# A layer kernel on one Trainium2 core: in fifteen of its seven-product pairs one matmul is made in two of fewer columns, or the third product comes second

## The chip, the cores and the metric

The kernel runs on one core of one Trainium2 chip. The metric is device time in microseconds (us). The kernel before was run three times without a profile: 875.72, 879.99 and 881.25 us, median 879.99. One more execution was profiled; the rows shown here are from that one.

A core has five engines that run side by side and wait for each other by semaphores: TensorE (PE in the profile) multiplies, VectorE (DVE) and ScalarE (ACT) work element by element, GpSimd (POOL) does small things and issues some DMAs, SyncE (SP) issues most DMAs. TensorE's work has two kinds of instruction: a weight load (PEld) puts a 128x128 block into the array, and the matmul behind it streams its columns through that block. A load runs beside the matmul before it.

## The reference, cut to what matters

A decoder layer on 512 tokens, 1024 wide: a feed-forward half step, a token mixer, a second feed-forward half step, a final norm.

```
x = x + 0.5 * swiglu_ffn(rmsnorm(x, ffn1_norm), w_gate1, w_up1, w_down1)
x = x + hybrid_mixer(rmsnorm(x, mix_norm), ...)
x = x + 0.5 * swiglu_ffn(rmsnorm(x, ffn2_norm), w_gate2, w_up2, w_down2)
y = rmsnorm(x, final_norm)

def swiglu_ffn(x, w_gate, w_up, w_down):      # w_gate, w_up: 1024 x 2816
    return (jax.nn.silu(x @ w_gate) * (x @ w_up)) @ w_down
```

Only `x @ w_gate` and `x @ w_up` are touched by the change.

## The kernel before

Every float32 operand of a product is split in a high and a low part, and a product is made as high*high + high*low + low*high. All matmuls have a 128x128 stationary block and 256 or 512 moving columns.

The 2816 features of a feed-forward step are 22 columns of 128, j = 0 to 21. Columns 0 and 1 (and 2 in the first step) are made plainly. For each later j the gate block and the up block together are a *pair*, and `seven_units` (line 452) makes the pair's four quarter results (two results, two halves of 256 tokens) in 7 half-size products instead of 8, by Strassen's scheme: sums of weight blocks (`block_hi`) by sums of token blocks (`sums`). Each product is one call of `mm_block` (line 310), 3 x 4 = 12 matmuls of 256 columns, so a pair has 84. The products go into three PSUM banks, in this order (B.., T. are weights, A.., S. token blocks):

```
("x","B11","A11"), ("z","T1","S1"), ("x","T2","S2"), ("w","B21","A12"),
("z","B22","S4"), ("x","T3","S3"), ("x","T4","A22")
```

Bank x is written by B11, and ScalarE then copies it out (`m1`, line 473) before T2 may add to it. In the same way ScalarE copies bank z (`m5`, line 477) between T1 and B22, and bank x again (`u2`, line 480) between T2 and T3. `c11`, `c12`, `c22`, `c21` add the pieces and apply silu (line 497 is `c21`'s).

`ffn` (line 940) strings the pairs together in three groups of 8, 8 and 6 columns. Each group ends with its down projection (`down_a_units`, banks pd, 512-column matmuls; the last group's is `down_b_units` or `final`). The pairs with 7 products are j = 3 to 21 in the first step and j = 2 to 21 in the second: 39 in all. `put(m[:6], 2)` lists a pair's first two products, then the last product (T4) of the pair before, then the other four. The last T4 of a group comes behind the first piece of the down projection.

The order of the instructions on each engine is a scheduler's: it takes units in the order of `run` and may move ready ones ahead of one that it believes will wait. ScalarE does, besides the copies, the casts of the weights to their high part (`slab_hi`, `block_hi`, lines 203 and 238), 1.05 us each for a whole block. VectorE makes the low parts (line 212) and the weight sums (lines 226 to 230).

Of the kernel before, what the change touches and what calls it, by code (L numbers as in the profile page):

```python
# [8 lines left out]
F32 = mybir.dt.float32  # L9
# [4 lines left out]
P = 128  # L14
# [4 lines left out]
T = 512  # L19
# [3 lines left out]
HT = 256  # L23
# [4 lines left out]
PLAIN = (3, 2)  # L28
BESIDE = (5, 9, 11, 13, 15, 18, 20)
ASIDE = 16  # L30
TAPS = 31
PR_NORM = 800
PR_CONV = -50
# [39 lines left out]
def layer_kernel(ctx: ExitStack, tc, x, gains, w_g1, w_u1, w_d1a, w_d1b, w_in,  # L73
                 chan, w_a, w_x, w_out, w_g2, w_u2, w_d2a, w_d2b, out):
    nc = tc.nc
    V, S, G, PE = nc.vector, nc.scalar, nc.gpsimd, nc.tensor
# [3 lines left out]
    sp = ctx.enter_context(tc.tile_pool(name="sp", bufs=2))  # L80
# [5 lines left out]
    def nm(s):  # L86
        uid[0] += 1
        return f"{s}_{uid[0]}"
# [4 lines left out]
    def bank(name):  # L93
        return pb.tile([P, T], F32, name=nm(name), tag="pb")
# [42 lines left out]
    def dve(us):  # L137
        clock["dve"] = max(clock["dve"], clock["pe"] - 3.0) + us
# [41 lines left out]
    def hl_tile(off):  # L180
        hl = wp.tile([P, 2 * D + 64], F32R, name=nm("hl"), tag="hl", bufs=HL_BUFS)
        return hl[:, off:off + 2 * D]
# [34 lines left out]
    def block_hi(s):  # L217
# [17 lines left out]
        n = HALF if s.kind == "b22" else D  # L235
        hl = hl_tile(ASIDE)
        s.hi, s.lo = hl[:, 0:n], hl[:, D:D + n]
# [69 lines left out]

    def mm_block(ps, b, a, first):  # L310
        (whi, wlo), (hhi, hlo) = b, a
        for i, (w, h) in enumerate(((whi, hhi), (whi, hlo), (wlo, hhi))):
            for k in range(4):
                PE.matmul(ps[:, 0:HT], w[:, k * P:(k + 1) * P], h[:, k, :],  # L314
                          start=(first and i == 0 and k == 0), stop=(i == 2 and k == 3),
                          skip_group_check=not first)

    pinned = [False]

# [100 lines left out]
    def ffn_units(acts, j, g, u_, parts):  # L420
        off = ASIDE if len(parts) == 2 else 0
        sg_, su_ = Slab(g, off=off), Slab(u_, off=off)
        box = {}

        def product(key, s, t0, n):
            box[key] = bank("p" + key)
            mm_feat(box[key][:, :n], s, t0, n)

        def gate_out(t0, n):
            box["s"] = sp.tile([P, T], F32, name=nm("sg"), tag="sg", bufs=2)  # L430
            S.activation(box["s"][:, :n], box["gate"][:, :n], AF.Silu)

        def up_out(t0, n):
            s, a = box["s"], acts[j]
            V.tensor_mul(s[:, :n], box["up"][:, :n], s[:, :n])
            S.copy(a[:, 0, t0:t0 + n], s[:, :n])
            V.tensor_sub(a[:, 1, t0:t0 + n], s[:, :n], a[:, 0, t0:t0 + n].bitcast(F32))
            dve(0.8 if n == 256 else 1.3)

        out_ = []  # L440
        for t0, n in parts:
            us = 5.44 * n / 512
            out_.append(Unit([sg_], us, lambda t0=t0, n=n: product("gate", sg_, t0, n),
                             lambda t0=t0, n=n: gate_out(t0, n), n == T))
            out_.append(Unit([su_], us, lambda t0=t0, n=n: product("up", su_, t0, n),
                             lambda t0=t0, n=n: up_out(t0, n), n == T))
        return out_
# [1 line left out]

    def seven_units(acts, j, g, u_, q):
        pair = {"gate": g, "up": u_}
        bg, bt, b2, bt2 = (Block(pair, k) for k in ("g", "t12", "b22", "t34"))
        right = {"B11": (bg, 0), "B21": (bg, 1), "T1": (bt, 0), "T2": (bt, 1), "B22": (b2, 0),
                 "T3": (bt2, 0), "T4": (bt2, 1)}
        box = {}
        h0, h1 = slice(0, HT), slice(HT, T)

        def product(to, b, a, first):  # L460
            if first:
                box[to] = bank("p" + to)
            blk, i = right[b]
            sl = slice(i * HALF, (i + 1) * HALF)
            mm_block(box[to], (blk.hi[:, sl], blk.lo[:, sl]), q[a], first)

        def evac(to, fn):
            with tc.high_priority(offset=PR_OUT):
                fn(box[to][:, 0:HT])

        def m1(ps):
            box["s"] = sp.tile([P, T], F32, name=nm("sg"), tag="sg", bufs=2)
            S.copy(box["s"][:, h0], ps)  # L473

        def m5(ps):
            box["m"] = sp.tile([P, T], F32, name=nm("um"), tag="um", bufs=2)
            S.copy(box["m"][:, h1], ps)

        def u2(ps):
            S.copy(box["m"][:, h0], ps)  # L480

        def c11(ps):
            V.tensor_add(box["s"][:, h0], ps, box["s"][:, h0])
            S.activation(box["s"][:, h0], box["s"][:, h0], AF.Silu)
            dve(0.42)

        def c12(ps):
            V.tensor_add(box["m"][:, h0], ps, box["m"][:, h0])
            dve(0.42)

        def c22(ps):
            V.tensor_add(box["m"][:, h1], ps, box["m"][:, h1])  # L492
            dve(0.42)

        def c21(ps):
            s, a = box["s"], acts[j]
            S.activation(s[:, h1], ps, AF.Silu)
            V.tensor_mul(s, s, box["m"])
            S.copy(a[:, 0, :], s)
            V.tensor_sub(a[:, 1, :], s, a[:, 0, :].bitcast(F32))  # L500
            dve(1.4)

        units = []
        for to, b, a, first, fn in (("x", "B11", "A11", True, m1), ("z", "T1", "S1", True, m5),
                                    ("x", "T2", "S2", False, u2), ("w", "B21", "A12", True, c11),
                                    ("z", "B22", "S4", False, c12), ("x", "T3", "S3", False, c22),
                                    ("x", "T4", "A22", False, c21)):
            units.append(Unit([right[b][0]], 1.41,
                              lambda to=to, b=b, a=a, first=first: product(to, b, a, first),
                              lambda to=to, fn=fn: evac(to, fn)))  # L510
        return units
# [86 lines left out]
    def zc_units(c, parts):  # L598
        off = ASIDE if len(parts) == 2 else 0
        sgt, sv = Slab(split=ws_in[4 + c], off=off), Slab(split=ws_in[c], off=off)  # L600
# [30 lines left out]
    def conv_out(c):  # L631
        return cv.setdefault(c // 2, slot([P, 2, T], "cv"))[:, c % 2, :]
# [15 lines left out]
    def conv_dve(c):  # L648
        acc, o = [bank("pc"), bank("pc")], conv_out(c)
        for j in range(TAPS):  # L650
            src, to = mx["ub"][:, c, j:j + T], acc[j % 2]
# [6 lines left out]
            else:  # L658
                V.scalar_tensor_tensor(out=o if j == TAPS - 2 else to, in0=src,  # L659
                                       scalar=par(c, P_DW + j), in1=to,  # L660
# [7 lines left out]
    def conv_pool(c):  # L668
        acc, o = slot([P, 2, T], "ca"), conv_out(c)
        for j in range(0, TAPS, 2):  # L670
            n = min(2, TAPS - j)
            to = acc if j == 0 else slot([P, 2, T], "cm")
# [248 lines left out]
    def do(fn):  # L921
        return [Unit([], 0.0, fn)]
# [13 lines left out]
    q1, q2 = {"name": "q1"}, {"name": "q2"}  # L936

    def ffn(a0, wg, wu, wd, q, plain, between=()):  # L940
        us, late, acts = [], [], [a0] + [Acts() for _ in GROUPS[1:]]
        js = iter(range(FT))

        def put(more, n):
            us.extend(more[:n] + late + more[n:])
            late.clear()

        ready = False
        for gi, n in enumerate(GROUPS):
            for i in range(n):  # L950
                j = next(js)
                if j < 2:
                    continue
                if j < plain:
                    put(ffn_units(acts[gi], i, wg[j], wu[j], [ALL]), 1)
                    continue
                if not ready:
                    us.extend(wait(q["name"]))
                    ready = True
                m = seven_units(acts[gi], i, wg[j], wu[j], q)  # L960
                m[4].aside = j in BESIDE
                if j == FT - 1:
                    put([m[k] for k in (0, 1, 2, 3, 5, 4, 6)], 1)
                else:
                    put(m[:6], 2)
                    late.append(m[6])
            if gi < 2:
                put(down_a_units(wd[gi], acts[gi], n), 1)
            if gi == 0:
                us.extend(between)  # L970
        assert not late
        return us, acts[2]

    for_later = [w_in[i] for i in range(16)] + [w_out[i] for i in range(8)]
    a1, a2 = Acts(), Acts()
    e = early_units(a1, w_g1, w_u1, wait("h11"))
    u = e[:1] + do(rest_of_x) + e[1:]
    u += do(lambda: sides.append(split_ahead(for_later, ws_in + ws_out)))
    f1, b1 = ffn(a1, w_g1, w_u1, w_d1a, q1, PLAIN[0], do(mixer_params))
    u += f1  # L980
    u += down_b_units(w_d1b, b1, then(2))
    u += do(mixer_inputs)
# [5 lines left out]
        (PR_NORM, norm_chain((t,), gains_of[3], f"h3{t // 2}" if t % 2 else None, q2))))  # L988
    u += wait("h30")
    u += early_units(a2, w_g2, w_u2, wait("h31"))  # L990
    f2, b2 = ffn(a2, w_g2, w_u2, w_d2a, q2, PLAIN[1])
    u += f2


# [105 lines left out]
```

## Time and profile before

| | us |
|---|---|
| three runs, median (lowest to highest) | 879.99 (875.72 to 881.25) |
| the profiled execution, its own time | 878.23 |
| its span, first to last instruction | 876.4 |
| PE busy in the span | 845.7 (96%) |
| DVE busy | 637.0 (73%) |
| ACT busy | 425.2 (49%) |

The rest of the time beside the span is 1.8 us. PE's busy time is that of matmul records that overlap each other (a 256-column matmul has a record of 0.28 us, and the next one starts 0.11 to 0.12 us after it). So the pace, start to start, is read from the starts of groups of matmuls in the timeline or from their count in a stretch, not from the busy share.

The program in the profile's time: first step 14 to 348 us, mixer 348 to 518, second step 518 to 836, end. The pairs with 7 products stand at 51 to 99, 144 to 221 and 266 to 328 us (first step) and at 551 to 609, 654 to 732 and 777 to 835 us (second step); between them are the down projections.

### The profile page before, as it was taken

The numbers are of one execution on the slowest core, as the hardware profiler recorded it, in microseconds if no ns is written. First come the engines' busy times: TensorE is split into PE (matmuls) and PEld (weight loads), VectorE is DVE, ScalarE is ACT, GpSimd is POOL, SyncE is SP. The second block draws the span as 40 slices with busy tenths as digits, with TensorE's granted clock in tenths as the row PEclk, the third lists the DMA queues.
The fourth block names the chain that finished last, engine by engine and source line by source line (L and its number), as shares of the span: only waits on it lengthen the run. The fifth ranks groups of instructions, "written<-read, shape, count | busy, mean of one in ns | idle before, by whom it ended". The sixth has DMA issues, their size and how long they took to land.

```text
span 876.4 us, 13745 instructions
## 1 busy us (share of the span) xinstructions
PE 845.7 (96%) x5568; PEld 768.7 (88%) x5568; DVE 637.0 (73%) x899; ACT 425.2 (49%) x677; POOL 89.7 (10%) x112
## 2 busy tenths in 40 slices
PE   7999999999998999999995999999999999999996
PEld 5999987999887998898783789999889999899985
DVE  5989655998666992659988569797547995558844
ACT  7656533656433661436652535555215654135633
POOL 2000011000111000209830010000000000000001
PEclk9999999999999999999998999999999999999998
DMA  7544689555898467555442021234312335223212
GB/s 273 162 134 170 220 309 334 193 193 170 304 325 306 145 230 275 207 202 191 145 156 84 4 93 49 95 104 134 127 49 96 101 117 164 77 73 97 102 44 96
DMA packets 36721, 139.12 MB, mean 159 GB/s; under 512 B 5041, under 2 KB 5169, under 8 KB 33970
## 3 DMA queue, kind: packets, MB, share of 16 engines
q1 hardware_dynamic: 29170, 112.04, 37.8%
q0 software_dynamic: 6912, 25.17, 7.5%
q10 hardware_dynamic: 576, 1.05, 0.3%
q8 instruction: 43, 0.70, 0.3%
q14 instruction: 20, 0.16, 0.1%
HBM read 110.98 MB, written 27.26 MB: 158 GB/s over the span
## 4 chain that ended last, share of the span: by engine, by line
PE 70%; issue 15%; DVE 5%; DMA 4%; ACT 3%; POOL 2%; SPq 0%; POOLq 0%; ACTq 0%; DVEq 0%
PE px L314 19%; PE pz L314 10%; PE pz L305 7%; PE pw L314 5%; PE pd L521 5%; PE pd L520 5%; PE pd L522 5%; PE pgate L305 3%; PE pup L305 3%; DVE pc L659 2%; DMA sraw<-in_w_out 2%; PE po L520 1%; PE po L521 1%; PE po L522 1%; PE pdl L521 1%
## 5 line engine op out<-in xcount | busy, mean ns | idle before, releaser
L212 DVE TENSOR_TENSOR hl<-raw,hl 128x1024 fp32r<-128x1024 f32 (+1 forms) x132 | 139.7, 1062 | 45.4 <-ACT hl L203 33.3
L314 PE MATMUL px<-sx,hl 128*128 128x256 f32 x936 | 122.7, 281 | 6.4 <-ACT sg L473 6.4
L314 PE MATMUL pz<-sx,hl 128*128 128x256 f32 x936 | 121.6, 280 | 0.0
L314 PEld LDWEIGHTS px<-sx,hl 128*128 128x128 f32 x936 | 115.3, 190 | 6.9 <-ACT sg L473 6.9
L520 PE MATMUL pd<-hl,act 128*128 128x512 f32 x304 | 118.7, 390 | 0.0
L521 PE MATMUL pd<-hl,act 128*128 128x512 f32 x304 | 118.4, 390 | 0.0
L522 PE MATMUL pd<-hl,act 128*128 128x512 f32 x304 | 118.4, 389 | 0.0
L212 DVE TENSOR_TENSOR hl<-tt,hl 128x1024 fp32r<-128x1024 f32 x78 | 94.9, 1217 | 30.3 <-ACT hl L238 30.3
L314 PEld LDWEIGHTS pz<-sx,hl 128*128 128x128 f32 x936 | 114.4, 189 | 0.0
L314 PE MATMUL px<-h_hi,hl 128*128 128x256 f32 x624 | 98.0, 280 | 0.0
L238 ACT CAST hl<-tt 128x1024 fp32r<-128x1024 f32 x78 | 81.8, 1052 | 27.8 <-PE pd L522 18.4
L314 PEld LDWEIGHTS px<-h_hi,hl 128*128 128x128 f32 x624 | 84.3, 189 | 1.2 <-DVE um L492 0.6
L203 ACT CAST hl<-raw 128x1024 fp32r<-128x1024 f32 x54 | 56.1, 1052 | 53.0 <-PE pd L522 42.3
L238 ACT CAST hl<-raw 128x1024 fp32r<-128x1024 f32 x78 | 65.1, 835 | 31.8 <-PE pd L522 26.3
L522 PEld LDWEIGHTS pd<-hl,act 128*128 128x128 f32 x304 | 57.1, 188 | 11.8
L520 PEld LDWEIGHTS pd<-hl,act 128*128 128x128 f32 x304 | 57.1, 188 | 11.5
L521 PEld LDWEIGHTS pd<-hl,act 128*128 128x128 f32 x304 | 57.1, 188 | 11.4
L305 PE MATMUL pz<-h_hi,hl 128*128 128x512 f32 (+1 forms) x320 | 64.9, 352 | 0.0
L305 PEld LDWEIGHTS pz<-h_hi,hl 128*128 128x128 f32 x320 | 51.8, 188 | 9.2 <-issue 1.9
L659 DVE SCALAR_TENSOR_TENSOR pc<-sx,ch,pc 128x512 f32<-128x512 f32 x84 | 56.9, 748 | 0.0
L291 DVE TENSOR_TENSOR slo<-sraw,shi 128x1024 fp32r<-128x1024 f32 x24 | 29.3, 1220 | 33.9 <-ACT shi L290 33.9
L290 ACT CAST shi<-sraw 128x1024 fp32r<-128x1024 f32 x24 | 25.2, 1051 | 52.7 <-DMA sraw<-in_w_in 30.3
(181 smaller groups left out, 1346.5 us busy)
## 6 DMA issues: line engine op xcount, KB each, us to landing
raw<-in_w_g SPq DMA_DIRECT2D x44, 512.0 KB, 3.6
raw<-in_w_u SPq DMA_DIRECT2D x44, 512.0 KB, 3.6
hl<-wsi SPq DMA_DIRECT2D x16, 1024.0 KB, 4.8
sraw<-in_w_in SPq DMA_DIRECT2D x16, 512.0 KB, 6.2
wsi<-shi POOLq DMA_DIRECT2D x16, 512.0 KB, 4.7
wsi<-slo POOLq DMA_DIRECT2D x16, 512.0 KB, 5.1
raw<-in_w_d1a SPq DMA_DIRECT2D x16, 512.0 KB, 4.3
raw<-in_w_d2a SPq DMA_DIRECT2D x16, 512.0 KB, 3.5
```

What stands on the lines that cost most here:

```text
L203: S.copy(s.hi, s.raw)
L212: V.tensor_sub(s.lo, s.raw, s.hi.bitcast(F32))
L238: S.copy(s.hi, s.raw)
L290: S.copy(hi, raws[-1])
L291: V.tensor_sub(lo, raws[-1], hi.bitcast(F32))
L305: PE.matmul(ps, w[:, k, :], h[:, k, t0:t0 + n], start=(i == 0 and k == 0), stop=(i == 2 and k == KT - 1))
L314: PE.matmul(ps[:, 0:HT], w[:, k * P:(k + 1) * P], h[:, k, :], start=(first and i == 0 and k == 0), stop=(i == 2 and k == 3), skip_group_ch ...
L520: PE.matmul(ps, ahi, whi, start=first, stop=False)
L521: PE.matmul(ps, ahi, wlo, start=False, stop=False)
L522: PE.matmul(ps, alo, whi, start=False, stop=last)
L659: V.scalar_tensor_tensor(out=o if j == TAPS - 2 else to, in0=src, scalar=par(c, P_DW + j), in1=to, op0=ALU.mult, op1=ALU.add)
```

## The change

`ffn` gets a table that names, by j, what is done in that pair. A number from 32 to 192 is a *cut*: in the pair's first product (B11) the second matmul (k = 1 of the first four) is made in two, the first with that many columns, the second with the rest of the 256; each has its own weight load of the same block. A 0 is a *swap*: the third product of the list, T2, is listed second, ahead of T1. There are 3 cuts and 1 swap in the first step, 8 cuts and 3 swaps in the second. The function `um` only lets whichever of `m5` and `u2` comes first make their tile.

```diff
+CUTS = ({3: 128, 4: 64, 5: 0, 6: 192},
+        {2: 0, 3: 192, 4: 128, 5: 64, 8: 64, 10: 32, 11: 0, 13: 128, 16: 128, 18: 0, 19: 64})
...
-    def mm_block(ps, b, a, first):
+    def mm_block(ps, b, a, first, cut=None):
         (whi, wlo), (hhi, hlo) = b, a
         for i, (w, h) in enumerate(((whi, hhi), (whi, hlo), (wlo, hhi))):
             for k in range(4):
-                PE.matmul(ps[:, 0:HT], w[:, k * P:(k + 1) * P], h[:, k, :],
-                          start=(first and i == 0 and k == 0), stop=(i == 2 and k == 3),
-                          skip_group_check=not first)
+                edges = [0, cut, HT] if cut and i == 0 and k == 1 else [0, HT]
+                for c0, c1 in zip(edges, edges[1:]):
+                    PE.matmul(ps[:, c0:c1], w[:, k * P:(k + 1) * P], h[:, k, c0:c1],
+                              start=(first and i == 0 and k == 0), stop=(i == 2 and k == 3),
+                              skip_group_check=not first)
...
-            mm_block(box[to], (blk.hi[:, sl], blk.lo[:, sl]), q[a], first)
+            mm_block(box[to], (blk.hi[:, sl], blk.lo[:, sl]), q[a], first,
+                     cut if b == "B11" else None)
...
+        def um():
+            if "m" not in box:
+                box["m"] = sp.tile([P, T], F32, name=nm("um"), tag="um", bufs=2)
+            return box["m"]
+
         def m5(ps):
-            box["m"] = sp.tile([P, T], F32, name=nm("um"), tag="um", bufs=2)
-            S.copy(box["m"][:, h1], ps)
+            S.copy(um()[:, h1], ps)
...
-                m = seven_units(acts[gi], i, wg[j], wu[j], q)
+                cut = cuts.get(j)
+                m = seven_units(acts[gi], i, wg[j], wu[j], q, cut)
                 m[4].aside = j in BESIDE
+                if cut == 0:
+                    m[1], m[2] = m[2], m[1]
```

A cut on TensorE, first step, pair 3 (the first row is the last matmuls of the plain column 2; px_73 is bank x, h_hi and h_lo the token block A11). Before:

```order
L305 MATMUL pup_66_546<-h_hi_76,hl_48_400 128x512 x8
L314 MATMUL px_73_588<-h_hi_76,hl_50_433 128x256 x4
L314 MATMUL px_73_588<-h_lo_77,hl_50_433 128x256 x4
L314 MATMUL px_73_588<-h_hi_76,hl_50_433 128x256 x4
L314 MATMUL pz_76_606<-sx0_52_461,hl_56_472 128x256 x12
```

and changed:

```order
L309 MATMUL pup_66_546<-h_hi_76,hl_48_400 128x512 x8
L320 MATMUL px_73_588<-h_hi_76,hl_50_433 128x256
L320 MATMUL px_73_588<-h_hi_76,hl_50_433 128x128 x2
L320 MATMUL px_73_588<-h_hi_76,hl_50_433 128x256 x2
L320 MATMUL px_73_588<-h_lo_77,hl_50_433 128x256 x4
L320 MATMUL px_73_588<-h_hi_76,hl_50_433 128x256 x4
L320 MATMUL pz_76_607<-sx0_52_461,hl_56_472 128x256 x12
```

One matmul of 256 columns became two of 128; nothing else moved here.

The swap on TensorE, first step, pair 5 (px_99 is its bank x, pz_102 or pz_105 its bank z; px_85 is bank x of pair 4, whose last product T4 is the rows from h_hi and h_lo into px_85; sx0 is S1, sx1 is S2). Before:

```order
L314 MATMUL px_99_815<-h_hi_76,hl_91_741 128x256 x4
L314 MATMUL px_99_815<-h_lo_77,hl_91_741 128x256 x4
L314 MATMUL px_99_815<-h_hi_76,hl_91_741 128x256 x4
L314 MATMUL pz_102_832<-sx0_52_461,hl_93_760 128x256 x12
L314 MATMUL px_85_692<-h_hi_76,hl_83_673 128x256 x4
L314 MATMUL px_85_692<-h_lo_77,hl_83_673 128x256 x4
L314 MATMUL px_85_692<-h_hi_76,hl_83_673 128x256 x4
L314 MATMUL px_99_815<-sx1_53_464,hl_93_760 128x256 x12
```

and changed:

```order
L320 MATMUL px_99_817<-h_hi_76,hl_91_743 128x256 x4
L320 MATMUL px_99_817<-h_lo_77,hl_91_743 128x256 x4
L320 MATMUL px_99_817<-h_hi_76,hl_91_743 128x256 x4
L320 MATMUL pz_105_868<-sx0_52_461,hl_93_762 128x256
L320 MATMUL px_85_693<-h_hi_76,hl_83_674 128x256 x3
L320 MATMUL px_99_817<-sx1_53_464,hl_93_762 128x256 x12
L320 MATMUL px_85_693<-h_hi_76,hl_83_674 128x256
L320 MATMUL px_85_693<-h_lo_77,hl_83_674 128x256 x4
L320 MATMUL px_85_693<-h_hi_76,hl_83_674 128x256 x4
L320 MATMUL pz_105_868<-sx0_52_461,hl_93_762 128x256 x11
```

Before, 24 matmuls stood between the end of B11 and T2, which needs ScalarE's copy of B11's result; now 4 do (one of T1, three of T4). The other swaps look the same, but for the second step's first pair, where there is no T4 yet and the four are of T1.

ScalarE at the same pair (sg_100<-px_99 is `m1`, um<-px_99 is `u2`, um<-pz is `m5`, the ACTIVATE is silu of pair 4's T4). Before:

```order
L473 COPY sg_100_828<-px_99_815 128x256
L477 COPY um_103_845<-pz_102_832 128x256
L497 ACTIVATE sg_86_705<-px_85_692 128x256
L238 CAST hl_105_864<-raw_84_689 128x1024
L499 CAST act_104_859<-sg_86_705 128x512
L480 COPY um_103_845<-px_99_815 128x256
```

and changed:

```order
L480 COPY sg_100_830<-px_99_817 128x256
L491 COPY um_102_846<-px_99_817 128x256
L508 ACTIVATE sg_86_707<-px_85_693 128x256
L242 CAST hl_104_865<-raw_84_690 128x1024
L510 CAST act_103_860<-sg_86_707 128x512
L488 COPY um_102_846<-pz_105_868 128x256
```

The copies of bank x and of bank z changed places around the silu and the two casts. VectorE, GpSimd and SyncE have the same instructions in the same order; TensorE has 11 matmuls and 11 loads more.

## Rows read from the trace of the kernel before

**Rows 1.** The page: span, busy time by engine, PE and its clock in 40 slices.

```profile
span 876.4 us, 13745 instructions
PE 845.7 (96%) x5568; PEld 768.7 (88%) x5568; DVE 637.0 (73%) x899; ACT 425.2 (49%) x677; POOL 89.7 (10%) x112
...
PE   7999999999998999999995999999999999999996
...
PEclk9999999999999999999998999999999999999998
```

**Rows 2.** Windows over the seven-product stretches (first column, us); columns in the first row.

```profile
core 0: us, PE busy (x) PEld busy (x) DVE busy (x) ACT busy (x) POOL busy (x), PEclk, DMA share, GB/s
51.20:98.80 47.60, 47.60 (x406) 47.60 (x405) 40.55 (x73) 30.76 (x51) 1.06 (x2) 1.00 0.40 132
150.20:220.00 69.80, 69.80 (x618) 69.80 (x618) 66.30 (x98) 44.62 (x76) 3.19 (x6) 1.00 0.56 193
278.40:317.60 39.20, 39.20 (x348) 39.20 (x347) 36.51 (x55) 24.45 (x42) 1.06 (x2) 1.00 0.45 152
551.60:608.00 56.40, 56.40 (x481) 56.40 (x481) 45.79 (x68) 33.17 (x58) 0.00 (x0) 1.00 0.30 95
654.60:732.00 77.40, 77.40 (x660) 77.40 (x659) 63.73 (x94) 45.68 (x78) 0.00 (x0) 1.00 0.32 102
777.40:832.00 54.60, 54.60 (x466) 54.60 (x465) 43.83 (x64) 31.38 (x55) 0.00 (x0) 1.00 0.29 98
```

**Rows 3.** Timeline of PE, 144 to 152.5 us: start, us, engine, line, tile, count, [idle before].

```profile
144.00 0.39 PE L522 MATMUL pd<-hl,act 128*128 128x512 f32 x1
144.22 0.64 PE L314 MATMUL px<-h_hi,hl 128*128 128x256 f32 x4
...
145.63 1.58 PE L314 MATMUL pz<-sx,hl 128*128 128x256 f32 x12
149.33 1.65 PE L314 MATMUL px<-sx,hl 128*128 128x256 f32 x12 [2.12 <-ACT sg L473]
150.82 0.62 PE L314 MATMUL pw<-h_hi,hl 128*128 128x256 f32 x4
...
152.18 0.50 PE L314 MATMUL pz<-sx,hl 128*128 128x256 f32 x3
```

**Rows 4.** Timeline of PE, 328 to 331 us.

```profile
328.89 0.40 PE L521 MATMUL pd<-hl,act 128*128 128x512 f32 x1
329.21 0.74 PE L314 MATMUL px<-h_hi,hl 128*128 128x256 f32 x4
329.79 0.62 PE L314 MATMUL px<-h_lo,hl 128*128 128x256 f32 x4
...
330.70 0.40 PE L522 MATMUL pd<-hl,act 128*128 128x512 f32 x1
330.93 0.40 PE L520 MATMUL pd<-hl,act 128*128 128x512 f32 x1
```

**Rows 5.** Chain that ended last: start, us, engine, bank, line, matmuls in the piece.

```profile
21.74 2.72 PE pgate L305 x24
25.33 2.83 PE pup L305 x24
```

**Rows 6.** Timeline of PE's weight loads, 24 to 25.4 us (128-column transposes, then 256-column matmuls).

```profile
24.20 0.89 PEld L348 LDWEIGHTS ptr<-ident,xn 128*128 128x128 f32 x8
25.06 0.42 PEld L305 LDWEIGHTS pup<-h_hi,hl 128*128 128x128 f32 x3
```

**Rows 7.** Timeline of all engines, 683.5 to 692.5 us (second step, pair 11).

```profile
683.68 0.64 PE L314 MATMUL px<-h_hi,hl 128*128 128x256 f32 x4
...
684.15 1.58 PE L314 MATMUL pz<-sx,hl 128*128 128x256 f32 x12
...
684.40 0.37 ACT L473 COPY sg<-px 128x256 f32<-128x256 f32 x1 [1.83 <-PE px L314]
...
686.50 0.64 PE L314 MATMUL px<-h_hi,hl 128*128 128x256 f32 x4
686.97 1.58 PE L314 MATMUL px<-sx,hl 128*128 128x256 f32 x12
687.17 0.38 ACT L497 ACTIVATE sg<-px 128x256 f32<-128x256 f32 x1 [1.04 <-PE px L314]
687.45 1.04 ACT L238 CAST hl<-raw 128x1024 fp32r<-128x1024 f32 x1
...
688.91 0.38 ACT L480 COPY um<-px 128x256 f32<-128x256 f32 x1
```

**Rows 8.** Timeline of ACT, 148 to 150 us: the copy that the matmul at 149.33 waits for.

```profile
148.92 0.36 ACT L473 COPY sg<-px 128x256 f32<-128x256 f32 x1
```

More of the change, by code (lines that the diff above doesn't have):

```diff
@@ L447, in ffn_units, with seven_units @@
         return out_
-    def seven_units(acts, j, g, u_, q):
+    def seven_units(acts, j, g, u_, q, cut=None):
         pair = {"gate": g, "up": u_}
@@ L473, in m1 @@
             S.copy(box["s"][:, h0], ps)
+        def um():
+            if "m" not in box:
+                box["m"] = sp.tile([P, T], F32, name=nm("um"), tag="um", bufs=2)
+            return box["m"]
         def m5(ps):
-            box["m"] = sp.tile([P, T], F32, name=nm("um"), tag="um", bufs=2)
-            S.copy(box["m"][:, h1], ps)
+            S.copy(um()[:, h1], ps)
         def u2(ps):
-            S.copy(box["m"][:, h0], ps)
+            S.copy(um()[:, h0], ps)
         def c11(ps):
@@ L936, in layer_kernel, with ffn @@
     q1, q2 = {"name": "q1"}, {"name": "q2"}
-    def ffn(a0, wg, wu, wd, q, plain, between=()):
+    def ffn(a0, wg, wu, wd, q, plain, cuts, between=()):
         us, late, acts = [], [], [a0] + [Acts() for _ in GROUPS[1:]]
@@ L978, in layer_kernel @@
     u += do(lambda: sides.append(split_ahead(for_later, ws_in + ws_out)))
-    f1, b1 = ffn(a1, w_g1, w_u1, w_d1a, q1, PLAIN[0], do(mixer_params))
+    f1, b1 = ffn(a1, w_g1, w_u1, w_d1a, q1, PLAIN[0], CUTS[0], do(mixer_params))
     u += f1
@@ L990, in layer_kernel @@
     u += early_units(a2, w_g2, w_u2, wait("h31"))
-    f2, b2 = ffn(a2, w_g2, w_u2, w_d2a, q2, PLAIN[1])
+    f2, b2 = ffn(a2, w_g2, w_u2, w_d2a, q2, PLAIN[1], CUTS[1])
     u += f2
```

## The prediction, made before the changed kernel was run

> **What bounds the kernel now.** I read the page first: PE is busy for 96% of the span, and its clock row stands at 9 nearly throughout [rows 1]. Then windows over the seven-product stretches: PE never stops in them, DVE has at least 2.6 us and ACT at least 14 us to spare in each, and the granted clock is 1.00, the 2.4 GHz level [rows 2]. These stretches are bound by TensorE; a change there is worth what it does to the pace of 256-column matmuls.
>
> The pace is read from counts. A count takes in about two matmuls that only reach over the edges, so I subtract 2. From 150.2 to 220.0 us: 69.80/616 = 113.3 ns from one matmul to the next; 278.4 to 317.6: 39.20/346 = 113.3. But 51.2 to 98.8: 47.60/404 = 117.8; 551.6 to 608.0: 56.40/479 = 117.7; 654.6 to 732.0: 77.40/658 = 117.6; 777.4 to 832.0: 54.60/464 = 117.7 [rows 2]. Same line, shape and clock: there are **two paces**, 4.4 ns apart. The first group of the first step and all of the second step have the slow one.
>
> Third, what goes before a change of pace. After 512-column matmuls the pairs start slow: from 144.22 to 145.63 twelve take 1.41 us, 117.5 ns each. At 149.33 PE has stood for 2.12 us, since T2 waited for ScalarE's copy of B11; T2's twelve take 1.49 us, and the next twelve, 150.82 to 152.18, take 1.36 us, 113.3 ns [rows 3], which lasts for the group. At 329.21 again 256 columns follow 512, but the start comes 0.32 us after the last one's instead of 0.23 (330.70 to 330.93), so PE stood for 0.09 us; and the eight from 329.79 to 330.70 go at 114 ns [rows 4]. The other way round, 24 matmuls at 2.72 us, then eight transposes of 128 columns, each paced by its weight load (0.86 us for eight, 108 ns), then 24 matmuls at 2.83 us [rows 5, 6]. So an empty TensorE that starts anew falls into the fast pace, and a busy one that changes column count falls into the slow one; either then stays. I take it that the pace hangs on how loads and matmuls lie to each other in time.
>
> **The change, part by part.** It gives TensorE a jolt in 15 pairs that stand where the pace is slow.
>
> *Swaps (4).* T2 now comes 4 matmuls behind B11 instead of 24. Pair 11 of the second step shows what that does. B11's last matmul starts at 683.68 + 3 x 0.118 = 684.03; T1 begins at 684.15; the copy runs from 684.40 to 684.77 [rows 7]. The load released by such a copy starts 0.05 us after its end (148.92 + 0.36 = 149.28, then 149.33) [rows 8, 3], so at 684.82. Four matmuls fill 684.15 to 684.62. PE stands for 0.20 us. T2's twelve then take 1.49 instead of 1.41 us, 0.08 more. Together 0.28 us a swap, 1.1 us for four. Lower bound 0.09 + 0.08, the shortest stop seen; upper bound 2.12 + 0.08, the stop with ScalarE busy [rows 3, 4]. I take 0.28, since in rows 7 ScalarE had been idle for 1.83 us before the copy.
>
> The swap also moves the copy of bank z behind a silu and two casts on ScalarE. From the last matmul of T4 (686.50 + 0.35 = 686.85) to the end of the copy in that place (688.91 + 0.38) it is 2.44 us [rows 7]. At the changed pair T2 ends at 684.82 + 1.49 = 686.31, T4's last nine at 687.33 (the last starts at 687.22), so the copy ends at 689.66. B22, which needs it, comes 11 matmuls of T1 and 12 of B21 later: 687.33 + 23 x 0.1133 = 689.94. Hidden, with 0.2 us to spare; without that cover it would stop PE again.
>
> *Cuts (11).* Two matmuls for one, 11 loads more. Parts of 32 to 224 columns are shorter than their load, so each should take a load's 108 ns [rows 6]: 2 x 0.108 - 0.118 = 0.10 us a cut, 1.1 us in all. Bounds: nothing, if the columns alone counted; 0.12 us each (two whole slow steps for one), 1.3 us, above.
>
> *What the pace gives back.* 4.4 ns for each matmul that goes fast. The slow stretches have 25 pairs of 84, less the four last T4s behind 512-column matmuls: 2,052 matmuls. Behind a swap, to the end of its group, stand 236 (first step, pair 5), 476, 404 and 320 (second step, pairs 2, 11 and 18), less T2's own twelve each: 1,388.
>
> A swap is the same wait, on the same instruction, as the stop at 149.33, and its 0.20 us lies between 0.09 and 2.12, which both led to the fast pace; I expect it to bring it. For a cut the trace has no row. The nearest is the transposes, which led to the slow pace, but there are eight of them in a row; two short matmuls are a smaller jolt. I take it that a cut leaves the pace as it finds it, and keep the other answers as rivals. Sum: 1.1 + 1.1 - 1,388 x 0.0044 = -3.9 us.
>
> Here the Trainium skill speaks against the change. In "TensorE: Matmul & The Clock Gate", in the step-by-step list of what each phase is for, it says that PE has two independent read ports, so that loading the next weights does not take read bandwidth from the running matmul; by that the relation of loads to matmuls would set no pace, and the sum would be the cost alone, +2.2 us. The trace doesn't agree as far as the two paces go: 113.3 and 117.7 ns with all else equal, changing at a stop.
>
> **The rivals.**
> A. *Cuts bring the fast pace too*, and leave it where it is. All 2,052 matmuls but a few go fast: 2.2 - 9.0 = -6.8 us. For it: any jolt might do. Against: the transposes.
> B. *Cuts throw the pace back to slow*, as transposes do. Then a swap pays only to the next cut: 57, 45, 141 and 57 matmuls behind T2, 300 in all: 2.2 - 1.3 = +0.9 us, slower than before. It decides when fewer than 500 matmuls (2.2/0.0044) go fast.
> C. *The pace belongs to something else*, and no jolt changes it. For it: the fast stretches are those with more DMA (shares 0.56 and 0.45 against 0.29 to 0.40) and a busier DVE [rows 2]. Against: it changed at one stop within one group. The change is then all cost: +2.2 us. By that rule of the Trainium skill it would come out the same.
> D. *The later copy of bank z comes too late*: one ScalarE cast (1.04 us, [rows 7]) more ahead of it uses up the 0.2 us and stops PE for up to 0.8 us, four times: 3.3 us on top, -0.6 us with the rest as forecast and about +4 us with B. It decides from 0.3 us of delay.
>
> **How the numbers follow.** My forecast 0.37, A 0.23, B 0.22, C 0.11, D 0.07. The profiled execution's 878.23 us less 3.9 is 874.3; the median of the runs is 1.8 us higher than that execution, and I put the time between, at 875.2. By A it is 871.4 to 873.2, by B 879.1 to 880.9, by C 880.4 to 882.2. The range goes from 870.5 (A, with the cuts at less than I priced them) to 881.5 (B whole, most of C), and leaves out the rest of C and half of D, with the runs' own spread. The forecast's own range is 873 to 877.5. One per cent is 8.8 us, about what a measurement of this kernel can tell from no change. No case reaches it: at most 2,052 x 0.0044 = 9.0 us are to be had, and 2.2 are paid. With the spread of the runs (875.72 to 881.25) on top I give faster by over 1% 0.08, within 1% 0.89, slower 0.03.
>
> **What would show it.** In the changed profile T2 of pairs 5, 2, 11 and 18 should have an idle time of about 0.2 us before it, put down to ScalarE's copy of bank x, and the matmuls behind it should come 113.3 ns apart; each cut should cost about 0.1 us. If the pace before a swap is fast already, a cut did it (A); if it is slow again behind the cut of pair 6 or pairs 3, 13 and 19, it is B; if it stays at 117.7 behind the stops, C. A wait of B22 for the copy of bank z would be D. Wrong altogether would be a stretch in which DVE or ACT, not TensorE, ends the waits, since then a faster pace would buy nothing.

## The result and the profile after

The changed kernel takes 874.46 us (median of 15 runs, 866.64 to 878.28) against 879.81 us before (15 runs, 874.27 to 884.28). The ratio is 0.9941, 95% interval 0.9919 to 0.9964: some 5 us faster, within one per cent. The forecast was 875.2 us in a range of 870.5 to 881.5, so time and direction came out as forecast. Two of the steps that led there were wrong, and a third, the price of a swap, was too small.

The page of the changed kernel, the lines that answer to [rows 1]:

```profile
span 873.9 us, 13774 instructions
PE 843.0 (96%) x5579; PEld 765.1 (88%) x5579; DVE 637.7 (73%) x899; ACT 425.4 (49%) x677; POOL 89.7 (10%) x112
```

Eleven matmuls and loads more, as the order said, and the other engines as before. The same windows view as [rows 2], with the columns named there, over the six groups. The second step's first group is split at 562.3, where its first cut stands; the windows 51.00, 656.40 and 777.00 each hold a swap and one or two cuts, 563.20 holds two cuts:

```profile
51.00:96.80 45.80, 45.57 (x402) 45.37 (x401) 39.44 (x68) 29.81 (x51) 1.06 (x2) 1.00 0.41 135
152.40:222.80 70.40, 70.40 (x600) 70.40 (x599) 63.48 (x93) 43.45 (x75) 3.19 (x6) 1.00 0.52 173
276.50:319.80 43.30, 43.30 (x370) 43.30 (x369) 40.30 (x58) 26.57 (x46) 1.60 (x3) 1.00 0.51 170
556.60:562.30 5.70, 5.70 (x51) 5.70 (x50) 2.73 (x5) 3.57 (x6) 0.00 (x0) 1.00 0.28 95
563.20:609.00 45.80, 45.80 (x406) 45.80 (x405) 39.12 (x57) 27.83 (x49) 0.00 (x0) 1.00 0.32 105
656.40:730.60 74.20, 73.97 (x652) 73.77 (x651) 62.65 (x92) 44.39 (x78) 0.00 (x0) 1.00 0.32 105
777.00:824.20 47.20, 46.97 (x415) 46.77 (x413) 40.08 (x59) 27.11 (x48) 0.00 (x0) 1.00 0.31 101
```

Read as in the prediction, count less two. The first step's first group and all of the second step behind its first cut are fast: 45.80/404 = 113.4 ns, and 114.2 to 114.5 where a swap's stop is in the window. That is what the change brought. But the first step's second and third group, fast in the profile before, are now slow: 70.40/598 and 43.30/368, 117.7 ns each. Nothing of the change stands in these two groups. Both begin with a stop at T2, as in [rows 3], and this time it left the slow pace. The same kernel profiled once more (`again`, below) has them fast and a span of 869.6 us; the profile before, 876.4 us, also has them fast. So which pace the two groups take is a matter of the execution, not of the change.

The two stops at T2 differ between executions too, and by as much. Here the first of them ends at 148.56; on ScalarE the copy that T2 waits for stands behind a cast that waited for a DMA:

```profile
146.25 1.04 ACT L294 CAST shi<-sraw 128x1024 fp32r<-128x1024 f32 x1 [5.19 <-DMA sraw<-in_w_in]
...
148.15 0.36 ACT L480 COPY sg<-px 128x256 f32<-128x256 f32 x1
```

Over the nine profiles with this layout of the weights (named below) the two stops together take from 5.1 to 10.3 us, as PE's wait for ScalarE's `sg`, and only the kernel with 39 cuts changes anything in their pairs. Between executions that makes 5 us, as much as the pace of the two groups can (4.9), so the time of a single run says little about the pace.

The changed kernel's waits of the matmuls (engine, line, waited for: us in all, times, longest):

```profile
PE px L320 <- ACT sg L480: 6.1, 2, 3.6
...
PE px L320 <- DVE um L503: 0.7, 3, 0.2
```

The first row is the same two stops as before the change ([rows 3] shows one). The second is new, and it is not the wait that I had named. Its place, in the second step's pair 11, on PE:

```profile
684.07 0.28 PE L320 MATMUL pz<-sx,hl 128*128 128x256 f32 x1
684.58 0.61 PE L320 MATMUL px<-h_hi,hl 128*128 128x256 f32 x3 [0.23 <-DVE um L503]
685.03 1.52 PE L320 MATMUL px<-sx,hl 128*128 128x256 f32 x12
```

and on VectorE:

```profile
682.97 1.22 DVE L216 TENSOR_TENSOR hl<-tt,hl 128x1024 fp32r<-128x1024 f32 x1
684.11 0.42 DVE L503 TENSOR_TENSOR um<-px,um 128x256 f32<-128x256 f32 x1
```

The swap lets three matmuls of T4 (of the pair before) move ahead of T2, and T4 adds into the bank that VectorE's `c22` (line 492 before, 503 now) must have read after T3. VectorE was still making a low part until 684.19, its read ended at 684.53, and the matmul that should have come at 684.07 + 0.11 came at 684.58: PE was about 0.4 us late (the row's 0.23 counts from the modelled end of the matmul before). T2 itself, at 685.03, then waited for nothing.

### The profile page after: what moved, and what is told of

It is laid out like the page before. It is cut to its first block, busy times and chain, and to the rows that moved or that the text cites. A ratio compares the mean times of both kernels' runs of the same rounds, so it can differ in the third digit from the quotient of the medians.

```text
span 873.9 us, 13774 instructions
## 1 busy us (share of the span) xinstructions
PE 843.0 (96%) x5579; PEld 765.1 (88%) x5579; DVE 637.7 (73%) x899; ACT 425.4 (49%) x677; POOL 89.7 (10%) x112
## 4 chain that ended last, share of the span: by engine, by line
PE 79%; DVE 8%; DMA 7%; ACT 4%; issue 1%; SPq 0%; POOL 0%; POOLq 0%; ACTq 0%; DVEq 0%
PE px L320 24%; PE pz L320 11%; PE pz L309 7%; PE pd L531 6%; PE pd L533 6%; PE pd L532 6%; PE pw L320 6%; DMA sraw<-in_w_in 3%; PE pgate L309 2%; PE pup L309 2%; DVE hl L216 2%; DVE pc L670 2%; DMA raw<-in_w_u 1%; PE po L531 1%; PE po L533 1%; PE po L532 1%
## 5 line engine op out<-in xcount | busy, mean ns | idle before, releaser
L531 PE MATMUL pd<-hl,act 128*128 128x512 f32 x304 | 118.7, 390 | 0.0
L320 PE MATMUL px<-h_hi,hl 128*128 128x256 f32 (+2 forms) x635 | 99.3, 279 | 0.7 <-DVE um L503 0.7
```

What stands on the lines that cost most here:

```text
L320: PE.matmul(ps[:, c0:c1], w[:, k * P:(k + 1) * P], h[:, k, c0:c1], start=(first and i == 0 and k == 0), stop=(i == 2 and k == 3), skip_gro ...
L531: PE.matmul(ps, ahi, whi, start=first, stop=False)
```

## The experiments

Each kernel is the changed one with another table, or the kernel before with one number changed, unless its diff says more. "Fast" and "slow" are 113.3 and 117.7 ns from one matmul to the next, read from windows (count less two).

**Cuts alone.** The swaps are taken out of the table.

```diff
-CUTS = ({3: 128, 4: 64, 5: 0, 6: 192},
-        {2: 0, 3: 192, 4: 128, 5: 64, 8: 64, 10: 32, 11: 0, 13: 128, 16: 128, 18: 0, 19: 64})
+CUTS = ({3: 128, 4: 64, 6: 192},
+        {3: 192, 4: 128, 5: 64, 8: 64, 10: 32, 13: 128, 16: 128, 19: 64})
```

> The 11 cuts alone, no swaps (every pair makes T1 ahead of T2 as before). Theory 1 (a cut brings the fast pace whatever stood before, a stop only by chance): the first step's first group goes fast from pair 3, the second step from pair 3, 8 and 16 on, 1,968 matmuls x 4.4 ns = 8.7 us less, 11 cuts x 0.11 = 1.2 us more: 7.5 us under the kernel before, if the first step's other two groups stand as they did in its profile; no stop of 0.2 to 0.4 us in pairs 5, 2, 11 and 18. Theory 2 (the swaps' stops do it, the cuts only keep it): the pace stays at 117.7 ns in the second step, and the time is 1.2 us over the kernel before.

Measured: 873.19 us (12 runs) against 877.97 us of the kernel before on the same chip (33 runs, the same for this and the next three kernels); ratio 0.9933, interval 0.9908 to 0.9958, which is 3.7 to 8.1 us less and holds the 7.5 of theory 1. Its windows:

```profile
52.00:95.00 43.00, 43.00 (x382) 43.00 (x380) 37.22 (x63) 27.52 (x48) 1.07 (x2) 1.00 0.41 135
160.00:220.00 60.00, 60.00 (x532) 60.00 (x531) 56.32 (x81) 39.51 (x69) 3.20 (x6) 1.00 0.55 187
288.00:328.00 40.00, 40.00 (x342) 40.00 (x342) 35.82 (x51) 25.59 (x44) 2.13 (x4) 1.00 0.48 157
...
566.00:611.00 45.00, 45.00 (x399) 45.00 (x398) 38.33 (x57) 27.31 (x48) 0.00 (x0) 1.00 0.31 103
659.00:731.00 72.00, 72.00 (x637) 72.00 (x636) 61.04 (x89) 42.73 (x75) 0.00 (x0) 1.00 0.31 103
780.00:825.00 45.00, 45.00 (x400) 45.00 (x398) 38.60 (x57) 26.57 (x46) 0.00 (x0) 1.00 0.33 106
```

Every group that has a cut is fast behind it (113.1 to 113.4 ns), with no swap anywhere; the last group loses the pace again in its last pair, behind this window (see the kernel with 39 cuts, below). Theory 2 falls. Of the two groups without a cut, the first went fast (60.00/530 = 113.2), the second slow (40.00/340 = 117.6).

**Swaps alone.**

```diff
+CUTS = ({5: 0}, {2: 0, 11: 0, 18: 0})
```

> The 4 swaps alone, no cuts. Theory 1 (a stop brings the fast pace only by chance; in the changed kernel's profile the stops at 275.5 and 555.5 us left it slow): some of the four swaps leave the pace at 117.7 ns; cost 3 x 0.5 + 0.3 = 1.8 us, the gain anything from 0 to 6.1 us. Theory 2 (a stop always brings it): 113.3 ns behind all four, 4.3 us under the kernel before. Both: a stop of about 0.4 us ahead of T4 of the pair before, put down to VectorE's read of bank x, in three of the four.

Measured: 876.3 us (12 runs), ratio 0.9988, interval 0.9955 to 1.002: no difference that can be told. The windows ahead of and behind the swaps of pairs 5, 2 (behind alone), 11 and 18:

```profile
56.00:70.00 14.00, 14.00 (x121) 14.00 (x121) 11.80 (x20) 10.12 (x16) 0.00 (x0) 1.00 0.29 93
72.00:98.00 26.00, 26.00 (x223) 26.00 (x222) 21.05 (x31) 16.56 (x28) 1.07 (x2) 1.00 0.46 153
558.00:610.00 52.00, 52.00 (x444) 52.00 (x443) 42.39 (x63) 30.77 (x53) 0.00 (x0) 1.00 0.29 101
660.00:684.00 24.00, 24.00 (x206) 24.00 (x205) 18.97 (x28) 14.15 (x26) 0.00 (x0) 1.00 0.33 96
690.00:732.00 42.00, 42.00 (x373) 42.00 (x372) 36.54 (x53) 27.10 (x47) 0.00 (x0) 1.00 0.32 103
780.00:796.00 16.00, 16.00 (x138) 16.00 (x138) 11.29 (x18) 9.23 (x17) 0.00 (x0) 1.00 0.28 87
802.00:825.00 23.00, 23.00 (x205) 23.00 (x205) 21.59 (x32) 15.60 (x27) 0.00 (x0) 1.00 0.34 107
```

117.6 stays 117.6 behind pair 5, and it is 117.6 behind pair 2; behind pairs 11 and 18 it falls to 113.2 and 113.3. Two of four: a stop does not bring the fast pace each time. The stops here were shorter than in the full change (in pair 11, 0.25 us from 686.48 to 686.73 where 0.12 is usual), probably because at the slow pace VectorE is less behind, which I did not test; the 0.4 us that I wrote down came in none.

**The changed kernel once more.**

> The changed kernel once more. Theory 1: behind all 11 cuts 113.3 ns again; behind the stops at T2 of the first step's pair 8 and of its third group's first pair, and of the second step's pair 2, either pace, so these may differ from the first profile (all three slow there). Theory of fixed order (the same program gives the same paces each time): exactly the same groups slow.

Measured: 874.5 us (10 runs), ratio 0.9964, interval 0.9931 to 0.9996. All 11 cuts have the fast pace behind them, as in the first profile; the two groups without a change are fast now (58.00/512 = 113.3 and 18.00/159 = 113.2 ns):

```profile
160.00:218.00 58.00, 58.00 (x514) 58.00 (x513) 54.51 (x79) 38.11 (x67) 3.19 (x6) 1.00 0.58 194
300.00:318.00 18.00, 18.00 (x161) 18.00 (x160) 17.60 (x25) 12.12 (x21) 0.66 (x2) 1.00 0.56 189
```

So the theory of fixed order falls: the same program comes out of the same stop fast in one execution and slow in another. Over the nine profiles with this layout (the kernel before, the changed one twice, and the six other kernels up to the price of a cut, below) the first step's two long stops at T2 came out fast 11 times and slow 7 times of 18.

The stop is not alone in this. In 11 of the 18 cases the granted clock fell to 0.50, the 1.2 GHz level, during the stop or soon behind it, and matmuls came 213 ns apart for a while; the groups went on fast in 8 of these 11 and in 3 of the other 7. In the kernel with the cuts alone the first stop left the slow pace (by the starts, 117 to 119 ns a matmul from 147.6 to 148.2 us), then the clock fell, and the pace was fast only after it had risen again:

```profile
148.40:151.40 3.00, 3.00 (x16) 3.00 (x15) 3.00 (x5) 1.32 (x2) 0.00 (x0) 0.50 0.75 305
```

No kernel here tells the clock's part from the stop's.

**One cut in each group.** No swap; a cut of 128 at the first pair of a group, at the second pair in the two groups whose first pair has the long stop.

```diff
+CUTS = ({3: 128, 9: 128, 17: 128}, {2: 128, 8: 128, 16: 128})
```

> One cut of 128 columns in each of the six groups, at its first pair (second pair in the first step's second and third group, whose first pair has a stop), no swaps. Theory 1 (a cut brings the fast pace whatever stood before, and nothing in a group throws it back): all six groups at 113.3 ns; against the kernel before 2,052 x 4.4 = 9.0 us less and 6 x 0.11 = 0.7 us more, so 8.3 us less, and more than that against those of its runs in which the first step's second or third group is slow (up to 4.9 us more). Theory 3 (each jolt throws dice, so several per group are needed): one or two of the six stay at 117.7 ns, and the time lies within 2 us of the changed kernel's.

Measured: 871.71 us (10 runs), ratio 0.9927, interval 0.9895 to 0.9959, 3.6 to 9.2 us less than before; 8.3 lies in it. All six windows behind the cuts:

```profile
53.00:97.00 44.00, 44.00 (x391) 44.00 (x390) 38.28 (x66) 28.76 (x50) 1.07 (x2) 1.00 0.42 133
166.00:225.00 59.00, 59.00 (x523) 59.00 (x523) 55.30 (x81) 38.51 (x67) 3.20 (x6) 1.00 0.56 189
287.00:320.00 33.00, 33.00 (x294) 33.00 (x293) 30.45 (x45) 20.56 (x37) 1.07 (x2) 1.00 0.44 145
557.00:611.00 54.00, 54.00 (x478) 54.00 (x478) 45.23 (x67) 32.78 (x58) 0.00 (x0) 1.00 0.31 102
658.00:731.00 73.00, 73.00 (x646) 73.00 (x646) 62.32 (x91) 44.16 (x77) 0.00 (x0) 1.00 0.33 105
778.00:824.00 46.00, 46.00 (x409) 46.00 (x408) 39.72 (x59) 26.94 (x47) 0.00 (x0) 1.00 0.34 104
```

All at 113.0 to 113.4 ns. Theory 3 falls: one cut per group does it, but for the last pair of the first step, where the pace is slow again from 324.4 us (below). In the third group the pace ahead of the cut was already fast. Its median lies 2.8 us under that of the changed kernel on the same chip, but the two intervals overlap, so that it is the better kernel is likely and not shown.

**What in a cut does it: a matmul more, or a short one?** At the six places of the last kernel nothing is cut; instead the first matmul of B11 is issued twice, the first time with all its columns or with 64.

```diff
+                if cut and i == 0 and k == 0:
+                    PE.matmul(ps[:, 0:cut], w[:, 0:P], h[:, 0, 0:cut],
+                              start=True, stop=False, skip_group_check=True)
+                PE.matmul(ps[:, 0:HT], w[:, k * P:(k + 1) * P], h[:, k, :],
...
```

> No cut and no swap; at the six places of the one-cut-per-group kernel the first matmul of B11 is issued twice with all its 256 columns (both start the sum anew, so the result is the same). Theory 1a (what brings the fast pace is that short matmuls leave TensorE waiting for the load, so load and matmul start together once): a full second matmul brings nothing, the groups of the second step and the first group of the first stay at 117.7 ns; each costs one matmul, 0.118 us. Theory 1b (any matmul and load more shifts the rhythm): 113.3 ns behind each.

> As the kernel with the full second matmul, but the one that is issued ahead has 64 columns, and no matmul is cut. Theory 1a: 113.3 ns behind all six, as behind a cut, at some 0.1 us each. Theory 1b: 113.3 ns here and with the full one alike. If it stays at 117.7 ns, it is the two parts of a cut that matter, not one short matmul.

With all columns (875.65 us, one run) the groups that were slow stay slow and the one that came fast out of the second step's plain columns stays fast:

```profile
52.00:98.00 46.00, 46.00 (x393) 46.00 (x392) 38.83 (x66) 29.32 (x50) 1.06 (x2) 1.00 0.40 131
555.00:606.00 51.00, 51.00 (x452) 51.00 (x451) 43.28 (x63) 31.66 (x55) 0.00 (x0) 1.00 0.33 106
655.00:728.00 73.00, 73.00 (x622) 73.00 (x621) 60.44 (x89) 42.77 (x75) 0.00 (x0) 1.00 0.32 103
778.00:825.00 47.00, 47.00 (x401) 47.00 (x401) 39.41 (x58) 26.63 (x47) 0.00 (x0) 1.00 0.32 102
```

117.6, 113.3, 117.7 and 117.8 ns. Theory 1b falls: a matmul and load more shift nothing. With 64 columns (882.26 us, one run, in which the two long stops take 10.3 us against 6.5 in the run with all columns):

```profile
52.00:95.00 43.00, 43.00 (x382) 43.00 (x381) 37.49 (x64) 27.78 (x47) 1.06 (x2) 1.00 0.41 137
162.00:226.00 64.00, 64.00 (x546) 64.00 (x545) 56.68 (x83) 40.55 (x70) 3.19 (x6) 1.00 0.50 173
290.00:328.00 38.00, 38.00 (x325) 38.00 (x324) 34.29 (x50) 24.23 (x41) 1.49 (x3) 1.00 0.44 141
563.00:617.00 54.00, 54.00 (x461) 54.00 (x460) 43.29 (x64) 31.82 (x56) 0.00 (x0) 1.00 0.33 101
665.00:737.00 72.00, 72.00 (x637) 72.00 (x637) 61.34 (x90) 43.41 (x76) 0.00 (x0) 1.00 0.34 104
786.00:828.00 42.00, 42.00 (x373) 42.00 (x372) 36.23 (x54) 25.60 (x44) 0.00 (x0) 1.00 0.34 102
```

Fast, slow, slow, slow, fast, fast. In the second and third group the pairs ahead of the short matmul had been fast, and it threw them back to 117.6. So theory 1a is right only in part: a short matmul can change the pace, but one alone changes it either way (of the four places in the slow pace or behind 512 columns three turned fast, and both that were fast turned slow); two in a row, as a cut makes them, gave the fast one each time. The two edits differ in more than that: the short matmul comes first in B11 and is 64 columns on top, while the parts of a cut come second and are 256 columns together. I have no kernel that says which of these differences counts.

**The price of a cut, and whether one ever throws the pace back.** A cut of 128 in all 39 pairs.

```diff
+CUTS = ({j: 128 for j in range(3, 22)}, {j: 128 for j in range(2, 22)})
```

> A cut of 128 columns in all 39 pairs, no swaps: the price of a cut, and whether one ever throws the fast pace back. Theory 1: 113.3 ns in all six groups from the first cut on, the fast pace back after each cut and after each stop; 39 cuts x 0.11 us = 4.3 us of cost against 9.0 us and up to 4.9 us of gain: 3 to 5 us slower than the kernel with one cut per group, 4 to 6 us faster than the kernel before. Theory 3 (each cut throws dice): some pairs at 117.7 ns.

Measured: 872.11 us (7 runs) against 878.38 (12), ratio 0.9937, interval 0.9913 to 0.9961. Behind all 39 cuts the pace is fast, also behind the two that follow a stop that came out slow. Counted over the five profiles with cuts at this layout (11, 11, 11, 6 and 39) that is 78 of 78, from 128/128, 64/192, 192/64 and 32/224 columns alike. But 55 of these cuts stood where the pace was fast already; 23 stood in the slow pace or right behind 512-column matmuls, and all 23 brought the fast one.

Without a cut there, the last pair of a step can throw the pace back. There the T4 of the pair before comes right behind B11; elsewhere T1 stands between. In all ten cases in which the fast pace reached this place, the first matmul of that T4 took 125 to 131 ns by the starts. Seven times the fast pace came back within a few matmuls; three times, with the cuts alone, the swaps alone and one cut per group, the rest of the group was slow, here with the cuts alone:

```profile
826.00:834.00 8.00, 8.00 (x70) 8.00 (x69) 5.17 (x7) 5.28 (x9) 0.00 (x0) 1.00 0.43 135
```

That is 8.00/68 = 117.6 ns, and costs some 0.3 us.

The price: from one cut to the next, 85 matmuls, it is 9.646 or 9.647 us in 25 of the 27 spans that hold just one pair (9.638 and 9.654 in the other two); 84 at 113.3 ns are 9.520. A cut costs 0.127 us. By that this kernel should be 33 x 0.127 = 4.2 us slower than the one with a cut per group; the ratios, each against its own runs of the kernel before, differ by 0.9 us with intervals of 2 to 3 us either way, so the runs neither show nor exclude it.

**Is it the place of the weights in SBUF?** The kernel before, with the start of the pairs' weights in their tile moved; the weights of columns 0 and 1 of each step and of the mixer's first two columns move with them, outside the windows below.

```diff
-ASIDE = 16
+ASIDE = 0
```

> The kernel before with the pairs' weights laid at the start of their tiles instead of 16 elements (64 bytes) on; no cut, no swap. If the slow pace comes of loads and matmuls meeting at places in SBUF (addresses), the paces change: another number than 117.7 or 113.3 ns, or another share of slow groups. If it is only a matter of when they start, both paces stay as they are, slow behind 512 columns.

> The kernel before with the pairs' weights 8 elements (32 bytes) into their tiles. Theory 4 (a repeat of 128 bytes): between 0 and 16, so a pace or paces of its own; if 113.3 ns is the floor set by a matmul's own columns, no pace is under it. Theory 6 (only whole steps of 64 bytes count): as 0, 120.0 ns.

> The kernel before (no cut, no swap) with the pairs' weights 32 elements (128 bytes) into their tiles instead of 16. At 0 elements every pair went at 120.0 ns, whatever went before; at 16 there are two paces. Theory 4 (loads and matmuls meet in SBUF by the place in a repeat of 128 bytes): 32 is as 0, 120.0 ns everywhere, about 10 us over the kernel before. Theory 5 (a longer repeat): something else, 113.3 ns everywhere at best, 5 to 9 us under the kernel before.

> The kernel before with the pairs' weights 48 elements (192 bytes) into their tiles. Theory 4 (a repeat of 128 bytes): as 16, that is slow (117.7 ns) behind 512-column matmuls and fast or slow behind stops, the same time as the kernel before within its spread. Theory 5: something else.

One run each: 889.69 us with 0, 883.36 with 8, 884.98 with 32, 885.16 with 48, against 878 to 880 for the kernel before beside them. The evidence is the pace. Windows of the second step's first and second group; with 0:

```profile
562.00:615.00 53.00, 53.00 (x444) 53.00 (x443) 41.36 (x62) 29.61 (x53) 0.00 (x0) 1.00 0.32 100
666.00:740.00 74.00, 74.00 (x619) 74.00 (x619) 59.47 (x87) 41.92 (x73) 0.00 (x0) 1.00 0.31 100
```

with 32:

```profile
558.00:610.00 52.00, 52.00 (x440) 52.00 (x439) 40.99 (x61) 29.43 (x52) 0.00 (x0) 1.00 0.32 102
664.00:734.00 70.00, 70.00 (x586) 70.00 (x585) 58.27 (x86) 39.55 (x69) 0.00 (x0) 1.00 0.31 99
```

With 0 it is 119.9 ns in both, and 120.0 in all six groups by the starts of the matmuls; with 32 it is 118.7 in one and 119.9 in the other (by the starts 118.7 in two groups and 120.0 in four); with 8 elements 118.3 in all six, with 48 elements 117.8 in all six. Nowhere but at 16 did a group go at 113.3, stops or not. Theory 4 falls with 32, which is not as 0, and theory 6 with 8.

**Does a cut bring the fast pace at 48 as well?** The kernel with one cut per group and `ASIDE = 48`.

> One cut of 128 columns per group with the weights 48 elements into their tiles, where all six groups stayed at 117.8 ns, stops or not. Theory 4 (the place counts in a repeat of 128 bytes, so 48 is as 16, and the two stops there missed the fast pace by chance): 113.3 ns behind the cuts, the time of the one-cut-per-group kernel. Theory 5 (48 is another place): no fast pace there, 117.8 ns behind the cuts too, or at most some other number.

884.13 us (one run, 878.55 before). Behind its cuts at 557.3 and 660.3:

```profile
560.00:612.00 52.00, 52.00 (x444) 52.00 (x443) 41.30 (x62) 29.68 (x53) 0.00 (x0) 1.00 0.32 102
664.00:736.00 72.00, 72.00 (x614) 72.00 (x613) 59.93 (x88) 42.03 (x73) 0.00 (x0) 1.00 0.32 103
```

117.6 ns, and 117.8 by the starts in the other groups too. The fast pace did not come there, as theory 5 had it, and theory 4 falls here too. So the pace depends on where the weights lie in their tile, and at 16 elements on what went before. That the place counts against that of the moving operand, or that it is a matter of how loads and matmuls happen to have started, is not shown: the moving operand was never moved.

## Why the prediction came out right, and where it was wrong

*What bounds the kernel: right.* TensorE never waits in the fast stretches either, but at the swaps; DVE and ACT kept up, and the gain shows in full. The second step's three groups, first to last start, take 56.7, 75.6 and 56.5 us instead of 57.8, 77.6 and 57.8, the first step's first group 47.0 instead of 47.9.

*Two paces that a jolt can change: right.* They differ by 4.4 ns, and rival C, that the pace belongs to other work, falls: the cuts changed it at each of 23 slow places. The Trainium skill has a rule in "TensorE: Matmul & The Clock Gate" ("Step-by-step: what each phase is for"), that loading weights does not take read bandwidth from the running matmul. By it the address of the weights should not matter to the pace. For these float32 operands it did: with the weights moved in their tile, the pace of the pairs went from 113.3 or 117.8 to 120.0 ns. Whether it is read bandwidth that the two share is not shown.

*"A cut leaves the pace as it finds it": wrong.* It brings the fast pace, 23 times of 23 where the pace was slow, and leaves it where it was fast, 55 of 55. This is rival A, to which I gave 0.23. I priced it by the nearest row, the transposes that led to the slow pace [rows 5, 6]; they are another kind of matmul (128 columns, which the sentence that all matmuls have 256 or 512 leaves out), and later profiles show a plain start behind transposes in either pace.

*"An empty TensorE that starts anew falls into the fast pace": wrong.* I had three changes of pace in one trace, and read a rule from two of them [rows 3, 4]. Over more executions it is 11 of 18 for the long stops, some with a fall of the clock besides, and 2 of 4 for the swaps alone. In the changed kernel's first profile the stop of pair 2 left the second step slow until the cut of pair 3 (117.7 ns by the starts; the window 556.60 to 562.30 is too short for its count).

*The price of a swap, 0.28 us: mis-sized.* Three of the four cost about 0.5 us (0.4 of stop and 0.1 of restart), the fourth 0.3: 1.8 us in all instead of 1.1. The term that I left out is T4's wait for VectorE. I had read from the order that three matmuls of T4 move ahead of T2 and counted them as cover, without asking what T4 itself waits for. The stop at T2 that I had worked out, 0.20 us, came only in pair 2, which has no T4 (0.21 us). Rival D, the later copy of bank z, did not come: no wait of B22 is in the changed kernel's profile.

*The price of a cut, 0.10 us: nearly right*, 0.127 measured, 1.4 us for the eleven. Its working was not: by the starts the second part comes 0.03 to 0.09 us behind the first, the later the more columns the first has, and not a load's 0.108; what makes up for it is the next whole matmuls, which come late (in 128/128, 0.06, 0.11 and 0.17 us from start to start).

*The sum.* With the measured terms it is 1.8 + 1.4 - about 1,960 x 0.0044 (all pairs of the four slow groups but those ahead of the first cut of the second step, and the few matmuls by which the pace settles) = -5.4 us, against -5.35 between the medians. My -3.9 came close because too few fast matmuls and too low a price partly cancelled, which is luck. The range held it since it reached to A. That the sum meets the medians to 0.1 us is luck as well: the interval goes from 3.2 to 7.1 us less, and not every execution has all four slow groups to win, since the second step came to its first pair fast, with no cut or swap ahead of it, in three of the nine profiles.

## What to carry to other kernels

Where an engine looks saturated, count its instructions over stretches: a busy TensorE may run the same matmul at two speeds, and only the count per microsecond shows it. A cheap jolt can be worth trying when a pace once taken is kept. One jolt per stretch was nearly enough here, and jolts made of stops cost more than the cuts and did not bring the pace each time. When work is moved up to fill a gap, ask what that work waits for, not only what it covers; and a rule about a state that is read from two or three events in one execution should be held against a second execution before it is priced.

## What the runs showed of the hardware that was not expected

- 128x256 fp32 matmuls, each with its own weight load, at the 2.4 GHz level, take from start to start 120.0 ns with the weights at an offset of 0 bytes in their tile, 118.3 at 32, 113.3 or 117.8 at 64, 118.7 or 120.0 at 128, and 117.8 at 192; at 64 either pace comes with the very same addresses.
- A pace once taken lasts for hundreds of matmuls (659 in a row in the second step before the change) and survives an added full-size matmul (6 of 6); within the pairs, apart from stops, cuts and single short matmuls, it changed only in the last pair of a step, 3 times of 10. Behind 512-column matmuls it was the slow one each time that neither a stop nor a short matmul followed.
- The same program takes either pace behind the same stop in different executions, worth up to 4.9 us. The stops themselves, which follow a DMA's landing, make another 5 us between executions (5.1 to 10.3 us in nine profiles). The runs of one kernel spread over 10 to 12 us; how much of that either makes in the runs without a profile is not shown.
